# Splitting the first scan projection's weights one stage earlier, in a diffusion backbone kernel on one core

## The chip, the cores and the metric

The kernel runs on one core of a Trainium2 chip, as one program. The metric is the device time of one execution in microseconds, smaller is better. The core has a matrix engine (PE, with its weight loads shown as PEld), a vector engine (DVE), a scalar engine (ACT) and a general engine (POOL), and queues that issue DMA transfers; nearly all of this kernel's are issued from SP.

## The reference

Two layers over 1024 latent tokens and 256 context tokens, model width 1024, all in float32. The even layer mixes by pooling and short convolutions. The odd layer has two branches of width 512: a bidirectional RWKV-7 scan over 8 heads of 64 and a Conformer convolution. The part in question:

```python
def odd_merge(y_c, z_c, p1, p2, z_d, w_out, dw_w, dw_b, ln_g, ln_b, grid):
    y_d = conformer_branch(p1, p2, dw_w, dw_b, ln_g, ln_b, "cols" if grid else "seq")
    y = jnp.concatenate([y_c * jax.nn.silu(z_c), y_d * jax.nn.silu(z_d)], axis=-1)
    return y @ w_out

def wkv_scan(r, w, k, v, a, bb, s0, reverse):
    def step(s, inp):
        r_t, w_t, k_t, v_t, a_t, b_t = inp
        sa = jnp.einsum("bhvk,bhk->bhv", s, a_t)
        s = s * w_t[:, :, None, :] + sa[..., None] * b_t[:, :, None, :] + v_t[..., None] * k_t[:, :, None, :]
        return s, jnp.einsum("bhvk,bhk->bhv", s, r_t)
```

The inputs of both branches and their gates (`r`, `k`, `v`, `z_c`, `p1`, `p2`, `z_d`) are column blocks of one projection, `h @ w_in`, of the modulated and normalised stream. Of these `p1`, `p2` and `z_d` aren't needed by the recurrence.

## The kernel before

**Split products.** A float32 value is kept as a rounded high half and a low half (value minus high half). A product of two such matrices is three matmuls into the same PSUM bank: low weights by high data, high by low, high by high. A weight tile of 128 x 1024 arrives raw by DMA in the one raw buffer `wr`; a cast on ACT makes the high half `wh`, a subtract the low half `wl`. There are two pairs of `wh` and `wl`, one in the pool `wp` and one in the pool `wpb`, used in turn by `(n - i) % 2` for the i-th tile of a list of n = 52 tiles.

**Stages.** `layer_even` is the even layer and its output projection. `odd_in` prepares the scan: it runs the projections for `r`, `k`, `v` of four head pairs j and four gate projections (matmuls at L1016), and works decay, keys and so on out of them on DVE, ACT and POOL; the results go to DRAM (`ARD`, `BKD`, `BTD`, `VTD`, `GD`, `ZCD`, ...). Here the low halves come by DMA from DRAM (`LOD`, made in the even layer), the high halves by a cast at L998. A gate projection's output is multiplied by `GD` at L1061 and stored to `ZCD` at L1063. `scan` does the recurrence in chunks of 64 tokens: 20 groups, each with key products (L1522) from `w` and `bk`, which DMAs at L1498 and L1505 bring in, inverses of small triangular blocks on POOL (L1420, L1421), and a chain of 40 dependent steps (L1741 on PE). Between these, as fill for PE, stand the remaining 12 projections (L1960, 48 matmuls each, 576 in all) and the output projection (L2102, 288 and L2307, 144 matmuls).

**Order.** The class `Lists` walks jobs (Python generators) that yield the engine and a planned duration of their next piece, or a resource or an event to wait for, and takes among those that are due the one with the best priority. It runs when the program is built; what comes out is a fixed order on each engine and in SP's queue, and on the chip each engine works through its list in that order, waiting on semaphores. So a job that becomes due at another time can reorder all later work. `odd_in` and `scan` each have their own such plan, one after the other.

**The first scan projection's weights.** In `odd_in`, `weights` (L980) loads tile after tile into `wr` and, for i < n, spawns `split_w` (L990), which takes the resource `w0` or `w1` (a free pair), has the low half loaded, casts the high half and frees `wr`. For i = n the tile is the first one of the scan, `self.wfirst`: it is loaded, and stays raw. In `scan`, `weights` (L1907) and `split_w` (L1920) go over the 12 projections and the output tiles: take `wr`, load (not for i = 0), then for each half of the tile cast on ACT (L1928) and subtract on DVE (L1934), then free `wr`, which lets the next tile's load be issued. The scan starts on the pair in `wp`; a second pair comes free much later.

```python
            for i, src in enumerate(self.worder):
                yield "R", "wr"
                at = L.got
                if i == 0:
                    raw = self.wfirst
```

Of the kernel before, what the change touches and what calls it, by code (L numbers as in the profile page):

```python
# [8 lines left out]
F32 = mybir.dt.float32  # L9
F32R = mybir.dt.float32r  # L10
AF = mybir.ActivationFunctionType
ALU = mybir.AluOpType
# [84 lines left out]
class Lists:  # L97
# [13 lines left out]
    def spawn(self, gen, prio):  # L111
        e = Job(gen, prio, self.cur.ready if self.cur else 0.0)
        self.advance(e)
        self.jobs.append(e)
        return e
# [6 lines left out]
    def note(self, key):  # L122
        self.ev[key] = self.cur.ready

    def free(self, name, what=None):
        self.res[name].append((self.cur.ready, what))
# [53 lines left out]
class Kern:  # L180
# [14 lines left out]
               wr=[0.0], w00=[0.0], w10=[0.0], w01=[], w11=[])  # L195
# [712 lines left out]
    def odd_in(self, es):  # L908
        tc, nc, A = self.tc, self.nc, self.A
# [67 lines left out]
        L = Lists(self.SL, self.LAT, self.RES2)  # L977
        spawn, note, free = L.spawn, L.note, L.free

        def weights():  # L980

            for i in range(i0 + 1, n + 1):
                if i > i0 + 1:
                    yield "R", "wr"
                    yield "S", 600, 3700
                    self.load(i)
                if i < n:
                    spawn(split_w(i), self.WP)

        def split_w(i):  # L990
            yield "R", f"w{(n - i) % 2}"
            p = (self.wp, self.wpb)[(n - i) % 2]
            raw = self.raws.pop(i)
            self.ready[i] = hi, lo = [p.tile([128, 8, 128], F32R, tag=t, name=t) for t in ("wh", "wl")]
            yield "S", 600, 300
            nc.sync.dma_start(out=lo.bitcast(F32), in_=self.LOD[i - n])
            yield "A", 950, 3100
            nc.scalar.copy(hi, raw)  # L998
            free("wr")
            note(("w", i))  # L1000
        used = [len(self.order) - self.NZ - 3 * NJ]
# [425 lines left out]
    def scan(self, es):  # L1427
# [454 lines left out]
        def rhs(src, k, b, c0, n):  # L1882
            return hn[src, k, b][:, c0:c0 + n]

        wts = [[[t[:, :4], t[:, 4:]] for t in (self.wp.tile([128, 8, 128], F32R, tag=t, name=t) for t in ("wh", "wl"))]]
        place = []

        def wt(a, k, ahead=0):
# [18 lines left out]
        def weights():  # L1907

            for i, src in enumerate(self.worder):
                yield "R", "wr"  # L1910
                at = L.got
                if i == 0:
                    raw = self.wfirst
                else:
                    raw = at or self.wp.tile([128, 8, 128], F32, tag="wr", name="wr")
                    yield "S", 600, 3700
                    self.wload(raw, src)
                spawn(split_w(i, raw, at), self.WP)

        def split_w(i, raw, at):  # L1920
            if i:
                yield "E", ("w", i - 1, 1)
            place.append((1 - place[-1]) if i and L.res["w01"] + L.res["w11"] + [1] * (1 in place) else 0)
            for q in range(2):
                yield "R", f"w{q}{place[i]}"
                (hi, lo), r = (t[q] for t in wts[place[i]]), raw[:, 4 * q:4 * q + 4]
                yield "A", 530
                nc.scalar.copy(hi, r)  # L1928
                if i < self.LOG:
                    yield "G", 1150  # L1930
                    nc.gpsimd.tensor_tensor(out=lo, in0=r, in1=hi.bitcast(F32), op=ALU.subtract)
                else:
                    yield "D", 610
                    nc.vector.tensor_tensor(out=lo, in0=r, in1=hi.bitcast(F32), op=ALU.subtract)  # L1934
                if q:
                    free("wr", at)
                note(("w", i, q))
# [485 lines left out]
```

## Time and profile before

| What | Value |
|---|---|
| Time, median of 3 runs | 1552.14 us (1549.43 to 1553.41) |
| Profiled execution, its own time | 1545.31 us |
| Its span in the profile | 1543.5 us |
| Granted TensorE clock, mean | 0.951 of full speed |
| Busy: PE, DVE, POOL, ACT | 1381.1, 993.9, 671.9, 637.0 us |

The busy times are those of one profiled execution; an engine counts as busy while it executes, not while it waits for a semaphore. The timelines give for each instruction its start from the span's start, its duration, its line and tiles, and in brackets how long its engine had been idle before it and what ended that. The chain of waits is followed back from the last instruction and names at each moment the work that the end was waiting for.

### The profile page before, as it was taken

The page shows a single profiled execution, that of the slowest core. Times are in us where ns is not written, and L with a number is a line of the kernel's source. Part 1 is how long each engine was busy: PE and PEld are TensorE (multiplying, and loading weights), DVE is VectorE, ACT ScalarE, POOL GpSimd, SP SyncE. Part 2 cuts the span into 40 slices and gives each one's busy share as a digit, 9 for nine tenths or more (in the row PEclk, how much of TensorE's full clock was granted, in tenths as well). Part 3 has the DMA queues.
Part 4 walks back from the last instruction along what each step waited for, and adds up shares of the span by engine and source line. Part 5 has one row for each costly group of instructions (what it writes and reads, how often), then busy time and mean ns, then how long its engine had stood idle before and what let it go on. Part 6 is the DMA issues. An engine that isn't in the chain of part 4 may idle for free.

```text
span 1543.5 us, 32203 instructions
## 1 busy us (share of the span) xinstructions
PE 1381.1 (89%) x12820; PEld 1084.7 (70%) x12820; DVE 993.9 (64%) x1681; ACT 637.0 (41%) x1257; POOL 671.9 (44%) x925
## 2 busy tenths in 40 slices
PE   6899999998999999899889878888998988886996
PEld 1578788887888778677667656676776666764775
DVE  3744464545822561279999964778688777788567
ACT  2551112122322552356556531344445643657534
POOL 1343535548455532135545421755557246406003
PEclk9899999999999999999999989899998998898999
DMA  7413433634253210537657775655655566774223
GB/s 266 152 66 123 169 131 129 213 137 162 70 174 124 67 65 33 147 99 218 199 169 226 224 253 150 159 141 150 168 141 151 165 157 173 218 225 127 86 86 109
DMA packets 174374, 232.32 MB, mean 151 GB/s; under 512 B 38832, under 2 KB 130352, under 8 KB 174096
## 3 DMA queue, kind: packets, MB, share of 16 engines
q1 hardware_dynamic: 172928, 228.69, 48.7%
q8 instruction: 101, 1.65, 0.5%
q10 hardware_dynamic: 1296, 1.57, 0.3%
q14 instruction: 49, 0.40, 0.1%
HBM read 164.93 MB, written 63.31 MB: 148 GB/s over the span
## 4 chain that ended last, share of the span: by engine, by line
PE 49%; DVE 17%; DMA 11%; POOL 10%; issue 6%; ACT 5%; SPq 2%; DVEq 0%; POOLq 0%; ACTq 0%
PE d L302 25%; PE d L2102 3%; PE d L1960 3%; PE d L1016 3%; DMA Bc<-ED 2%; POOL X L1421 2%; POOL tmp L1420 2%; DMA bk<-BKD 2%; PE sc L1522 2%; PE d L944 2%; DMA ad<-in_ada_e 1%; POOL wl L268 1%; PE pa L1741 1%; PE pr L458 1%; DVE Z L1090 1%
## 5 line engine op out<-in xcount | busy, mean ns | idle before, releaser
L302 PE MATMUL d<-sx,wh 128*128 128x512 f32 x1152 | 365.8, 399 | 2.4 <-DVE sx L528 1.3
L302 PEld LDWEIGHTS d<-sx,wh 128*128 128x128 f32 x1152 | 220.5, 192 | 54.2 <-POOL sx L398 1.8
L302 PE MATMUL d<-sx,wl 128*128 128x512 f32 x576 | 233.1, 405 | 12.3 <-POOL wl L268 9.1
L1420 POOL TENSOR_TENSOR tmp<-X,Bc 128x120 f32<-128x120 f32 (+2 forms) x300 | 120.0, 400 | 195.0 <-DMA Bc<-ED 172.6
L1016 PE MATMUL d<-sx,wh 128*128 128x512 f32 x512 | 162.8, 400 | 0.0
L268 POOL TENSOR_TENSOR wl<-wr,wh 128x1024 fp32r<-128x1024 f32 x37 | 98.8, 2671 | 139.4 <-ACT wh L267 139.4
L629 DVE SCALAR_TENSOR_TENSOR junk<-wra,cb 128x1024 bf16<-128x1024 f32 x56 | 108.3, 1934 | 75.5 <-DMA wra<-in_ada_o 51.0
L1960 PE MATMUL d<-sx,wh 128*128 128x512 f32 x384 | 139.3, 430 | 0.0
L302 PEld LDWEIGHTS d<-sx,wl 128*128 128x128 f32 x576 | 110.4, 192 | 38.7 <-POOL wl L268 10.1
L1421 POOL TENSOR_TENSOR X<-X,tmp 128x120 f32<-128x120 f32 (+2 forms) x300 | 124.8, 416 | 23.5
L1016 PEld LDWEIGHTS d<-sx,wh 128*128 128x128 f32 x512 | 98.6, 193 | 22.1 <-issue 2.7
L1016 PE MATMUL d<-sx,wl 128*128 128x512 f32 x256 | 112.9, 441 | 0.0
L302 PE MATMUL d<-sc,wh 128*128 128x256 f32 x576 | 104.1, 281 | 0.0
L1960 PE MATMUL d<-sx,wl 128*128 128x512 f32 x192 | 83.8, 437 | 9.8 <-DVE wl L1934 9.8
L1981 DVE SCALAR_TENSOR_TENSOR acc<-hc,vec,acc 128x960 f32<-128x960 f32 (+14 forms) x120 | 90.0, 774 | 1.1
L302 PEld LDWEIGHTS d<-sc,wh 128*128 128x128 f32 x576 | 88.8, 190 | 1.4
L267 ACT CAST wh<-wr 128x1024 fp32r<-128x1024 f32 x37 | 38.7, 1046 | 119.8 <-PE d L302 64.5
L1960 PEld LDWEIGHTS d<-sx,wh 128*128 128x128 f32 x384 | 74.5, 200 | 16.5 <-issue 0.2
L302 PE MATMUL d<-sc,wl 128*128 128x256 f32 x288 | 81.0, 281 | 0.0
L1522 PE MATMUL sc<-w,bk 64*128 64x128 f32 (+1 forms) x640 | 55.4, 311 | 20.4 <-issue 9.1
L1522 PEld LDWEIGHTS sc<-w,bk 64*128 64x128 f32 x640 | 46.8, 210 | 28.2 <-issue 25.2
L1536 DVE TENSOR_TENSOR w<-sc,cstb 64x256 f32<-64x256 f32 x80 | 33.8, 422 | 47.2 <-PE sc L1522 28.5
(381 smaller groups left out, 2880.6 us busy)
## 6 DMA issues: line engine op xcount, KB each, us to landing
wr<-in_in_o SPq DMA_DIRECT2D x32, 512.0 KB
wr<-in_in_e SPq DMA_DIRECT2D x24, 512.0 KB
wra<-in_ada_o SPq DMA_DIRECT2D x24, 512.0 KB
BKD<-bk SPq DMA_DIRECT2D x40, 256.0 KB
BTD<-X SPq DMA_DIRECT2D x20, 512.0 KB
bk<-BKD SPq DMA_DIRECT2D x40, 256.0 KB
Bc<-ED SPq DMA_DIRECT2D x20, 512.0 KB
bkt<-BTD SPq DMA_DIRECT2D x40, 256.0 KB
```

Source lines behind the costliest of these rows:

```text
L267: self.nc.scalar.copy(hi, raw)
L268: self.nc.gpsimd.tensor_tensor(out=lo, in0=raw, in1=hi.bitcast(F32), op=ALU.subtract)
L302: self.nc.tensor.matmul(ps[:, :n], lhsT=w[a][:, k, :], rhs=rhs(src, k, b, c0, n), start=(i == 0), stop=(i == len(seq) - 1))
L629: nc.vector.scalar_tensor_tensor(out=junk, in0=w, scalar=1.0, in1=cb[:, s, :], op0=ALU.mult, op1=ALU.mult, accum_out=dst[:, s:s + 1])
L1016: nc.tensor.matmul(ps, lhsT=w[a][:, k, :], rhs=rhs(s, k, b, c0, m), start=(q == 0), stop=(q == len(seq) - 1))
L1420: g.tensor_tensor(out=t, in0=X[:, :, j:j + 1].to_broadcast([128, 8, m]), in1=B[:, j, :, j + 1:16] if j < 8 else B2[:, j - 8, :, j - 7:8], ...
L1421: g.tensor_tensor(out=X[:, :, j + 1:16], in0=X[:, :, j + 1:16], in1=t, op=ALU.add)
L1522: nc.tensor.matmul(ps[h][:, d, i, h:h + 1] if ctx else ps[h][:, d, i], lhsT=bk[R[h], c, d, i], rhs=w[R[h], c, d, sl, i, :], start=True, st ...
L1536: nc.vector.tensor_tensor(out=w[o, c, :, 2 * h], in0=ps[h][o, :, :, h], in1=ma[o].unsqueeze(2).to_broadcast([64, 2, 2, 64]), op=ALU.mult)
L1960: nc.tensor.matmul(ps, lhsT=wt(a, k), rhs=rhs("x", k, b, c0, 512), start=(i == 0), stop=(i == len(seq) - 1))
L1981: nc.vector.scalar_tensor_tensor(out=acc[:, o], in0=hc[:, q], scalar=w, in1=acc[:, o], op0=ALU.mult, op1=ALU.add)
L2102: nc.tensor.matmul(ps, lhsT=wt(a, at), rhs=ysrc(k, b, c0), start=(i == 0), stop=(i == len(seq) - 1))
```

## The change

`split_w` in `odd_in` now also runs for i = n: it waits for the pair of buffers in `wp` that the last but one gate projection frees, casts the whole tile on ACT, and subtracts on POOL (there is no stored low half for this tile); `wr` is free after that. In `scan`, the first pair of `wts` is that tile's. For i = 0, `weights` takes no `wr` and `split_w` only notes that the halves are there. Thus the two ACT casts of half a tile, and the two DVE subtracts, of the first scan projection are gone from the scan, and the raw buffer is free when its plan begins.

```diff
@@ odd_in @@
-                if i < n:
-                    spawn(split_w(i), self.WP)
+                spawn(split_w(i), self.WP)
 
         def split_w(i):
+
             yield "R", f"w{(n - i) % 2}"
             p = (self.wp, self.wpb)[(n - i) % 2]
             raw = self.raws.pop(i)
             self.ready[i] = hi, lo = [p.tile([128, 8, 128], F32R, tag=t, name=t) for t in ("wh", "wl")]
-            yield "S", 600, 300
-            nc.sync.dma_start(out=lo.bitcast(F32), in_=self.LOD[i - n])
+            if i < n:
+                yield "S", 600, 300
+                nc.sync.dma_start(out=lo.bitcast(F32), in_=self.LOD[i - n])
             yield "A", 950, 3100
             nc.scalar.copy(hi, raw)
+            if i == n:
+                yield "G", 2310
+                nc.gpsimd.tensor_tensor(out=lo, in0=raw, in1=hi.bitcast(F32), op=ALU.subtract)
             free("wr")
             note(("w", i))
@@ scan @@
-        wts = [[[t[:, :4], t[:, 4:]] for t in (self.wp.tile([128, 8, 128], F32R, tag=t, name=t) for t in ("wh", "wl"))]]
+        wts = [[[t[:, :4], t[:, 4:]] for t in self.ready[len(self.order)]]]
@@ scan, weights @@
             for i, src in enumerate(self.worder):
-                yield "R", "wr"
-                at = L.got
-                if i == 0:
-                    raw = self.wfirst
-                else:
+                raw = at = None
+                if i:
+                    yield "R", "wr"
+                    at = L.got
                     raw = at or self.wp.tile([128, 8, 128], F32, tag="wr", name="wr")
                     yield "S", 600, 3700
                     self.wload(raw, src)
@@ scan, split_w @@
             for q in range(2):
                 yield "R", f"w{q}{place[i]}"
+                if i == 0:
+                    note(("w", i, q))
+                    continue
                 (hi, lo), r = (t[q] for t in wts[place[i]]), raw[:, 4 * q:4 * q + 4]
```

The engines' orders move as follows; the new lines of the changed kernel lie 4 to 6 lines lower than the old ones (L1960 is now L1966, L1934 is L1940, L1498 is L1502, L1505 is L1509). Numbers behind a tile's name are versions of it; `w` and `bk` are operands of the key products, `sx` the halves of the input stream, `wh` and `wl` the weight halves.

On PE, where the preparation's last matmuls end and the scan's first projection begins, before:

```order
L1016 MATMUL d<-sx_131,wl 128x512
L1016 MATMUL d<-sx_132,wh 128x512
L1016 MATMUL d<-sx_131,wh 128x512
L1960 MATMUL d<-sx_117,wl 128x512 [waits DVE_49]
L1960 MATMUL d<-sx_118,wh 128x512 [waits Activation_49]
L1960 MATMUL d<-sx_117,wh 128x512
L1960 MATMUL d<-sx_119,wl 128x512
```

and the same place now:

```order
L1020 MATMUL d<-sx_131,wl 128x512
L1020 MATMUL d<-sx_132,wh 128x512
L1020 MATMUL d<-sx_131,wh 128x512
L1966 MATMUL d<-sx_117,wl 128x512 [waits DVE_49,Pool_49]
L1966 MATMUL d<-sx_118,wh 128x512
L1966 MATMUL d<-sx_117,wh 128x512
L1966 MATMUL d<-sx_119,wl 128x512
```

The first matmul's DVE semaphore stood before for the low half's subtract; now it stands for the eviction L1051 (now L1055) of the last preparation bank, and the POOL semaphore for the new subtract. The waits for halves inside the first 48 matmuls are gone. The 32 fill matmuls that stood ahead of the key products of group 0 are now 60, the 76 ahead of those of group 1 now 100, the 116 ahead of group 2 now 144, the 160 ahead of the chain's first step 188; at the chain's step 30 all 576 have been issued in both, and 303 fill matmuls follow the chain's last step instead of 297.

On SP's queue at the start of the scan, before:

```order
L1441 DMA cstb<-in_cstb 128x408
L1498 DMA w_7354<-ARD 64x128 x8
L294 DMA wr<-in_in_o 128x1024
L1505 DMA bk<-BKD 128x2x256 x2
L1498 DMA w_7355<-ARD 64x128 x8
L1498 DMA w_7356<-ARD 64x2x128 x8
L1571 DMA ED_7334<-eb 128x128
L1571 DMA ED_7335<-eb 128x64
L1505 DMA bk<-BKD 128x2x256 x2
```

and now:

```order
L1445 DMA cstb<-in_cstb 128x408
L294 DMA wr<-in_in_o 128x1024
L1502 DMA w_7357<-ARD 64x128 x8
L1502 DMA w_7358<-ARD 64x128 x8
L1509 DMA bk<-BKD 128x2x256 x2
L1502 DMA w_7359<-ARD 64x2x128 x8
L294 DMA wr<-in_in_o 128x1024
L1502 DMA w_7360<-ARD 64x2x128 x8
L1575 DMA ED_7338<-eb 128x128
L1575 DMA ED_7339<-eb 128x64
L1509 DMA bk<-BKD 128x2x256 x2
```

The raw load of the second projection's weights is now the first after `cstb`; group 0's `bk` stands behind the `w` transfers of two groups instead of one, and group 1's `bk` behind one more raw load and eight more `w` transfers.

On DVE, between the chain's steps 35 and 36, on the way to the subtract of a late weight tile, before:

```order
L2180 SCALAR_TENSOR_TENSOR stat<-part,stat 128x256
L1846 TENSOR_TENSOR sq<-sq,ms 128x256
L1848 SCALAR_TENSOR_TENSOR rs<-sq,rs 128x256
L2188 TENSOR_TENSOR cv<-cv,stat 128x512
L1859 SCALAR_TENSOR_TENSOR dv<-dv,vec,rs 128x256
L2188 TENSOR_TENSOR cv<-cv,stat 128x512
L2166 TENSOR_TENSOR stat<-part 128x256
L1863 SCALAR_TENSOR_TENSOR dv<-dv,vec,ms 128x256
L1865 TENSOR_TENSOR dv<-dv,sq 128x256
L1934 TENSOR_TENSOR wl<-wr,wh 128x512
```

and now:

```order
L2181 TENSOR_TENSOR stat<-stat,part 128x256
L2165 SCALAR_TENSOR_TENSOR cv<-d,cv 128x512 x2
L1940 TENSOR_TENSOR wl<-wr,wh 128x512
L2185 TENSOR_TENSOR part<-part,stat 128x256
L2186 SCALAR_TENSOR_TENSOR stat<-part,stat 128x256
L2194 TENSOR_TENSOR cv<-cv,stat 128x512
L1846 TENSOR_TENSOR ms<-ms,sq 128x256
L2194 TENSOR_TENSOR cv<-cv,stat 128x512
```

The subtract of the second half stood behind the norm operations of the scan's and the convolution's output (`rs`, `dv`, `cv`); it now stands ahead of most of them. On ACT the casts of half a tile fall from 32 to 30, those of a whole tile at L998 (now L999) rise from 15 to 16, and there are four activation table loads more (one each at L1835, L2018, L2170 and L2192). On POOL the one new row, the subtract, stands behind the last `kd` product (L1215) and ahead of the copies to `PT` (L1235). The counts on PE and SP are the same in both.

## Rows read from the trace of the kernel before

**Rows 1.** The page's first part: busy us, share of span, instructions.
```profile
PE 1381.1 (89%) x12820; PEld 1084.7 (70%) x12820; DVE 993.9 (64%) x1681; ACT 637.0 (41%) x1257; POOL 671.9 (44%) x925
```

**Rows 2.** Timeline of PE: start us, us, what, count, [idle before <-releaser].
```profile
913.37 0.63 PE L1016 MATMUL d<-sx,wh 128*128 128x512 f32 x2
923.59 0.79 PE L1960 MATMUL d<-sx,wl 128*128 128x512 f32 x1 [9.59 <-DVE wl L1934]
...
927.25 0.39 PE L1960 MATMUL d<-sx,wl 128*128 128x512 f32 x1
...
932.01 0.39 PE L1960 MATMUL d<-sx,wl 128*128 128x512 f32 x1
...
934.35 0.66 PE L1522 MATMUL sc<-w,bk 64*128 64x64 f32 x8 [0.15 <-DMA bk<-BKD]
```

**Rows 3.** Timeline of DVE, the same stretch.
```profile
907.91 1.23 DVE L1061 TENSOR_TENSOR ex<-ex 128x1024 f32<-128x1024 f32 x1 [2.59 <-DMA ex<-GD]
...
914.66 0.69 DVE L1051 SCALAR_TENSOR_TENSOR ex<-ex,d 128x512 f32<-128x512 f32 x1 [0.90 <-ACT ex L1049]
920.80 1.23 DVE L1061 TENSOR_TENSOR ex<-ex 128x1024 f32<-128x1024 f32 x1 [5.45 <-DMA ex<-GD]
...
922.87 1.27 DVE L1934 TENSOR_TENSOR wl<-wr,wh 128x512 fp32r<-128x512 f32 x2
```

**Rows 4.** Timeline of SP's queue at the scan's start: time to issue.
```profile
922.47 0.38 SPq L1441 DMA_DIRECT2D cstb<-in_cstb  x1
923.08 5.11 SPq L1498 DMA_DIRECT2D w<-ARD  x8
928.29 0.53 SPq L294 DMA_DIRECT2D wr<-in_in_o  x1
928.86 0.94 SPq L1505 DMA_DIRECT2D bk<-BKD  x2
929.85 10.15 SPq L1498 DMA_DIRECT2D w<-ARD  x16
```

**Rows 5.** Chain of waits, transfers on it: start us, us to landing, what.
```profile
915.67 5.04 DMA ex<-GD
...
929.34 4.97 DMA bk<-BKD
...
942.80 7.12 DMA wr<-in_in_o
...
1275.15 2.10 DMA sv<-VTD
```

**Rows 6.** Timelines of ACT and POOL in the preparation.
```profile
886.70 1.06 ACT L998 CAST wh<-wr 128x1024 fp32r<-128x1024 f32 x1
...
900.88 0.59 ACT L1330 COPY X<-t 128x512 f32<-128x512 f32 x1 [0.89 <-DMA BTD<-X]
...
909.64 1.27 POOL L1256 TENSOR_TENSOR kb<-kd 128x256 f32<-128x256 f32 x1 [3.12 <-DMA BON<-kb]
```

**Rows 7.** The page's costliest groups: busy us, mean ns | idle before.
```profile
L268 POOL TENSOR_TENSOR wl<-wr,wh 128x1024 fp32r<-128x1024 f32 x37 | 98.8, 2671 | 139.4 <-ACT wh L267 139.4
```

**Rows 8.** Windows: us, each engine's busy us, then PEclk, DMA share, GB/s.
```profile
923.60:927.30 3.70, 3.70 (x10) 2.93 (x11) 0.53 (x1) 0.00 (x0) 0.29 (x1) 0.56 0.53 158
988.00:1316.50 328.50, 290.33 (x5840) 225.62 (x5840) 250.83 (x560) 152.36 (x383) 185.38 (x471) 0.93 0.60 156
1378.00:1416.00 38.00, 25.59 (x340) 18.00 (x341) 31.50 (x67) 23.95 (x55) 22.60 (x55) 0.87 0.48 140
```

**Rows 9.** Timelines of PE and DVE late in the scan.
```profile
1402.54 0.79 PE L2102 MATMUL d<-y,wl 128*128 128x512 f32 x1 [8.63 <-DVE wl L1934]
...
1393.48 0.41 DVE L1842 TENSOR_TENSOR ms<-ms,sq 128x256 f32<-128x256 f32 x1
...
1401.77 0.71 DVE L1934 TENSOR_TENSOR wl<-wr,wh 128x512 fp32r<-128x512 f32 x1
```

**Rows 10.** Groups kept apart by shape: busy us, mean ns | idle before.
```profile
L1835 ACT ACT_TABLE_LOAD x5 | 6.4, 1283 | 0.1
```

## Prediction, made blind

> **What bounds the kernel now.** I began with the busy shares: TensorE (PE) works 89% of the span [rows 1], so a microsecond in which PE stands still, with work left that only it can do, is a microsecond of the end unless a chain of dependences ends it later. Next I read PE's timeline where the preparation of the scan ends and the scan begins [rows 2]. The last matmul of the preparation starts at 913.37, and the scan's first matmul at 923.59, after 9.59 us of idling until a low half of the weights (`wl`, L1934) is there. VectorE's (DVE) timeline says why it is late [rows 3]: the subtract that makes it is at 922.87, behind the last gate multiply L1061 at 920.80, which waits 5.45 us for a load of `GD`; that load leaves SP's queue at 915.67 and takes 5.04 us [rows 5]. The weights themselves have long been in the raw buffer. So the first projection is held by its place in DVE's order, and by nothing that it needs.
>
> SP's queue is the second thing to see [rows 4]. After `cstb` at 922.47 it issues the eight `w` transfers of key group 0 (5.11 us for eight issues), then the second projection's raw weights, then the two `bk` transfers; the second `bk` leaves at 929.34 and takes 4.97 us to land [rows 5], and the first key products run at 934.35 [rows 2]. From 988, where the chain of the groups has begun, to 1316.5 PE is busy 290.33 of 328.50 us [rows 8], some 88%: neither full, which would make every earlier microsecond count, nor idle enough for the chain alone to set the pace. That is the doubt of this forecast.
>
> **The change part by part.** The profiled execution took 1545.31 us (span 1543.5); the median is 1552.14, 0.44% above. I sum differences against the profile and put them on the median.
>
> *1. The gap.* The first projection's pair is ready in the preparation. In the changed order its first matmul waits for the last eviction of the preparation (L1051) and for the new POOL subtract; the eviction is at 914.66 and lasts 0.69 us, with 0.05 to start: PE starts at 915.4 instead of 923.59, **−8.2 us**. After the gap PE's first matmuls are slow: ten start between 923.59 and 927.25, in 3.66 us, nine intervals of 0.407 us, while the 21 intervals to 932.01 take 4.76 us, 0.227 each [rows 2]; the granted clock there is 0.56 of full speed [rows 8], about the lower level (1.2 of 2.4 GHz). With PE idle for 1.8 us instead of 9.6 I take these nine at 0.227: 9 × 0.18 = **−1.6 us**.
>
> *2. The next weights.* First projection: 48 × 0.227 = 10.9 us, so it ends at 926.3. The second one's raw weights are issued once `cstb` is, at about 922.9 instead of 928.29, and land 5.04 to 7.12 us later (the shortest and longest 512 KB transfer on the chain) [rows 5], at 927.9 to 930.0; half a cast, about 0.6, and a subtract of 0.7 [rows 9] give 929.3 to 931.4. PE waits 3.0 to 5.1 us there: a **new wait**, which takes some of the gap's gain back. Then twelve matmuls (2.7 us) to at most 934.1, about 932 at the early end.
>
> *3. The keys of group 0.* The same order puts one raw load and sixteen `w` issues ahead of the two `bk`: 922.9 + 0.53 + 10.15 [rows 4] + 0.5 = 934.1 for the second `bk`, instead of 929.34, 4.8 us later. Landing by the row of 4.97 gives 939.1, by the shortest row of a small transfer (2.10, `sv`) [rows 5] 936.2; I take 4.97, which is the same transfer. The first key products then come 4.75 us later (939.1 against 934.35), but with 60 fill matmuls behind them instead of 32: 28 × 0.227 = 6.4 us of work done. Net −1.6. PE has nothing else there, so it idles some 5 us before them and may drop to the lower clock again: up to +1.6 back, which leaves 0.
>
> The Trainium skill ("DMA: Bandwidth & Descriptors", section "Anatomy of one DMA — SWDGE (gpsimd) path") gives a transfer a fixed cost of about 2.0 us plus its bytes at 436 GB/s; that page fits it for transfers issued from GpSimd, these leave SP's queue. As an estimate by that page 256 KB take 2.6 us, the keys would come 2.4 us late, and the net would be −4.0; the trace's row for this transfer is nearly twice that, and it decides.
>
> *4. Groups 1 and 2.* Group 1's keys have one raw load and eight `w` more ahead (0.53 + 5.11 = 5.6 us [rows 4]) against 24 fills done earlier (5.4): +0.2. Group 2's: 5.6 later against 28 fills (6.4): −0.8. The mean of the three, (−1.6 + 0.2 − 0.8)/3 = **−0.7 us**, is my value for the start. Its ends: −9.8 (terms 1 and 1b kept whole, the chain never late) and +5.6 (the chain of groups sets the pace, each comes by what SP is later, and the fills done ahead buy nothing).
>
> *5. The fill runs out earlier or not.* In the changed order PE has 28 fills more behind it at chain step 0, 12 to 20 at steps 18 to 21, none at step 30, where all 576 are done in both. The lead is thus spent within the chain: fewer fills stand between its steps. It is a gain where PE is the later one, and idle time where the chain is. The 88% above [rows 8] fit both, so I take the middle, that is, term 4 as it stands.
>
> *6. Late in the scan.* PE waits 8.63 us, to 1402.54, for a `wl` whose subtract stands at 1401.77, behind a row of norm operations on DVE that began at 1393.48 [rows 9]. The changed order puts that subtract ahead of most of them: −8.6 at best, if nothing follows that is as late; PE is busy 25.59 of 38.00 us there [rows 8], so something else is late too, and six fills more remain after the last chain step (6 × 0.227 = +1.4). On the other side the order holds four ACT table loads more; such a load takes 1283 ns [rows 10]: +5.1 if each lies on the path. Middle of −8.6 and +5.1: **−1.75 us**.
>
> *7. What lies under cover.* The new whole cast on ACT (1.06 [rows 6]) comes where ACT has 0.89 of idle ahead of L1330 [rows 6]; what is left, 0.2, meets DVE's 2.59 before L1061 [rows 3]. The new POOL subtract takes 2.67 us (same form [rows 7]) and stands ahead of the operations that lead to 909.64, where POOL idles 3.12 [rows 6]; without that cover it would cost up to 2.7 through the keys of the last preparation. The two DVE subtracts and two ACT casts that go (1.27 on DVE [rows 3]) end nothing by themselves.
>
> Sum: −0.7 − 1.75 = −2.5 us; on the median 1552.14 − 2.5 = 1549.6, put at **1549.5 us**.
>
> **The rivals.** *A, little is left (my forecast):* as above; within ±4.66 us of the median (0.3%, about what a measurement of this kernel can tell from no change). For it: terms 2 and 3, a wait for weights and one for `bk` where there was one gap. That PE doesn't start early at all (the POOL subtract not done by 915.4) also ends here, near 1552.
>
> *B, the lead survives:* the 28 fills count whole, 6.4 us, or all of term 1, 9.8: 1552.1 − 6.4 to − 9.8 − (0 to 1.75) = 1540.6 to 1545.7, and down to 1534 if term 6 gives its 8.6 too. For it: PE's 89% [rows 1]. Against: 38 us of idling from 988 on [rows 8], which says that fills alone don't fill the chain.
>
> *C, slower:* SP's queue decides. Each early group's `bk` stands behind more `w` issues (0.63 each), the chain of groups is the later one from group 0 on, and starts 4.75 to 5.6 us later with nothing to make it good; then 1556.9 to 1557.7, with the table loads (+5.1) up to 1562.8. It decides as soon as PE's idling between the chain's steps grows by more than the 6.4 us of fill that it no longer has to do there. For it: the keys already wait for `bk` before [rows 2].
>
> **How the numbers follow.** A 0.40, B 0.37, C 0.23: A because the two new waits each take back a known share; B before C because PE's share is high and the fills done early are real work. The time is A's, 1549.5. The range takes in most of B (to 1541.0) and of C (to 1559.0) and leaves about 0.1 out on each side; A's own range is 1547.5 to 1556.8. Faster by over 0.3% is B, slower is C.
>
> **What would show it.** Term 1: the first L1960 matmul (a few lines lower in the new code) at 915 to 916, and no run of 0.4 us intervals behind it. Term 2: a PE wait of 3 to 5 us for `wl` after 48 matmuls. Term 3: the first key products at 936 to 940, with PE idle ahead of them for `bk`. Terms 4 and 5: the chain's first step no earlier than 986, and PE's idle time between steps larger than before by about the start's gain. Term 6: no 8.63 us wait near 1400, and ACT table loads on the chain of waits. The forecast is wrong if the chain's first step comes 6 us or more earlier and stays so (B), or later than 992 (C).

## The result and the profile after

The changed kernel is slower: 1558.11 us, median of 19 runs (1544.20 to 1571.17), against 1549.61 for the kernel before in the same comparison. The ratio is 1.0055, interval 1.0039 to 1.0072: 8.5 us lost, where 2.5 us were forecast to be gained. Single executions lie up to 14 us from their kernel's median (the one profiled of after took 1563.56, that of before 1545.31), so the 18.25 us between the two profiled ones overstate the loss; what follows rests on places that come back in several traces.

Up to the first keys the start went much as worked out. PE's timeline of after (start us, us, instruction, [idle before <-what ended it]), against [rows 2]:

```profile
913.02 0.63 PE L1020 MATMUL d<-sx,wh 128*128 128x512 f32 x2
915.14 0.47 PE L1966 MATMUL d<-sx,wl 128*128 128x512 f32 x1 [1.50 <-DVE ex L1055]
...
928.46 0.50 PE L1966 MATMUL d<-sx,wl 128*128 128x512 f32 x1 [2.17 <-DVE wl L1940]
...
937.01 1.12 PE L1526 MATMUL sc<-w,bk 64*128 64x64 f32 x8 [4.07 <-issue]
938.34 1.12 PE L1526 MATMUL sc<-w,bk 64*128 64x64 f32 x8 [0.21 <-DMA bk<-BKD]
...
991.60 1.06 PE L1745 MATMUL pa<-sv,w 128*64 128x64 f32 x16
```

PE starts at 915.14 instead of 923.59, waits 2.17 us for the next weights, and stands idle again ahead of the first keys, whose second eight run at 938.34 instead of 934.35, and take 1.12 us instead of 0.66. The last row is the chain's step 0: 991.60, later than before, although 28 fill matmuls more have been done. The same row of the kernel before:

```profile
987.89 0.69 PE L1741 MATMUL pa<-sv,w 128*64 128x64 f32 x16
```

SP's queue of after at the scan's start, against [rows 4]:

```profile
921.95 0.38 SPq L1445 DMA_DIRECT2D cstb<-in_cstb  x1
922.39 0.77 SPq L294 DMA_DIRECT2D wr<-in_in_o  x1
923.38 10.07 SPq L1502 DMA_DIRECT2D w<-ARD  x16
933.50 1.10 SPq L1509 DMA_DIRECT2D bk<-BKD  x2
...
947.54 0.81 SPq L1575 DMA_DIRECT2D ED<-eb  x2
...
955.34 1.36 SPq L1582 DMA_DIRECT2D Bc<-ED  x2
```

The last row, `Bc`, is the load from which POOL makes the first inverses. It left at 950.55 before:

```profile
950.55 1.33 SPq L1578 DMA_DIRECT2D Bc<-ED  x2
```

Later in the scan, the waits view of PE (what waited for what: us in total, times, longest), first of before from step 0 on:

```profile
PE d L2102 <- DVE wl L1934: 8.6, 1, 8.6
...
PE pa L1746 <- DVE rh L1743: 4.1, 6, 1.4
...
PE d L2152 <- DVE stat L2149: 0.5, 2, 0.2
```

and of after:

```profile
PE pa L1750 <- DVE rh L1747: 13.9, 7, 5.0
...
PE d L2158 <- DVE stat L2155: 10.4, 2, 9.9
```

The late wait for `wl` [rows 9] is gone, as the order had said; two others stand in its place: for `rh` (the chain's own copy out of PSUM, queued on DVE behind other work) and for `stat`. The windows (us, busy PE, PEld, DVE, ACT, POOL, then the granted clock) from step 0 to the end, of before and of after:

```profile
987.90:1543.50 555.60, 473.38 (x8053) 366.59 (x8052) 414.20 (x888) 274.81 (x656) 240.89 (x585) 0.92 0.54 151
```

```profile
991.60:1561.50 569.90, 470.24 (x8026) 365.42 (x8024) 406.28 (x877) 280.48 (x661) 237.65 (x586) 0.89 0.51 146
```

PE is without work for 82.2 us of the one and 99.7 of the other, and its matmuls, 27 fewer, take nearly as long at the lower granted clock. That PE idles more comes back in the other traces: 80.7 to 87.9 us from step 0 on in the eight of the old order that leave out no matmul behind step 0 (before, b2, e1, e6, e9, e11, e12, e16), 88.9 to 99.7 in the six of the changed one (after, e2, e3, e4, e13, e15), 11 us more in the mean.

### The profile page after: what moved, and what is told of

Its sections match the earlier page's. It is cut to its first block, busy times and chain, and to the rows that moved or that the text cites. A ratio compares the mean times of both kernels' runs of the same rounds, so it can differ in the third digit from the quotient of the medians.

```text
span 1561.5 us, 32197 instructions
## 1 busy us (share of the span) xinstructions
PE 1385.8 (89%) x12820; PEld 1091.0 (70%) x12820; DVE 998.6 (64%) x1679; ACT 641.9 (41%) x1260; POOL 666.8 (43%) x926
## 4 chain that ended last, share of the span: by engine, by line
PE 49%; DVE 16%; DMA 11%; POOL 9%; issue 7%; ACT 6%; SPq 3%; DVEq 0%; POOLq 0%; ACTq 0%
PE d L302 24%; PE d L1966 4%; PE d L1020 4%; DMA Bc<-ED 3%; PE d L2108 3%; POOL tmp L1424 2%; POOL X L1425 2%; PE d L944 2%; PE sc L1526 1%; POOL wl L268 1%; DMA cv<-CVD 1%; PE pa L1769 1%; DMA ad<-in_ada_e 1%; PE pa L1750 1%; DVE acc L1987 1%
## 5 line engine op out<-in xcount | busy, mean ns | idle before, releaser
L629 DVE SCALAR_TENSOR_TENSOR junk<-wra,cb 128x1024 bf16<-128x1024 f32 x56 | 113.2, 2021 | 73.9 <-DMA wra<-in_ada_o 49.1
L1966 PE MATMUL d<-sx,wh 128*128 128x512 f32 x384 | 142.0, 441 | 0.0
L1425 POOL TENSOR_TENSOR X<-X,tmp 128x120 f32<-128x120 f32 (+2 forms) x300 | 119.5, 398 | 23.5
L1020 PEld LDWEIGHTS d<-sx,wh 128*128 128x128 f32 x512 | 99.7, 195 | 22.2 <-issue 2.7
L302 PEld LDWEIGHTS d<-sc,wh 128*128 128x128 f32 x576 | 88.9, 190 | 1.4
L1966 PE MATMUL d<-sx,wl 128*128 128x512 f32 x192 | 85.6, 446 | 3.7 <-DVE wl L1940 2.2
L1966 PEld LDWEIGHTS d<-sx,wh 128*128 128x128 f32 x384 | 76.6, 206 | 16.8 <-issue 0.4
L267 ACT CAST wh<-wr 128x1024 fp32r<-128x1024 f32 x37 | 38.7, 1047 | 120.6 <-PE d L302 72.2
L1219 POOL TENSOR_TENSOR kd<-kd,Z 128x512 f32<-128x512 f32 x20 | 29.5, 1477 | 77.7 <-DVE kd L1215 77.7
```

The costliest lines, as they stand in the source:

```text
L267: self.nc.scalar.copy(hi, raw)
L302: self.nc.tensor.matmul(ps[:, :n], lhsT=w[a][:, k, :], rhs=rhs(src, k, b, c0, n), start=(i == 0), stop=(i == len(seq) - 1))
L629: nc.vector.scalar_tensor_tensor(out=junk, in0=w, scalar=1.0, in1=cb[:, s, :], op0=ALU.mult, op1=ALU.mult, accum_out=dst[:, s:s + 1])
L1020: nc.tensor.matmul(ps, lhsT=w[a][:, k, :], rhs=rhs(s, k, b, c0, m), start=(q == 0), stop=(q == len(seq) - 1))
L1425: g.tensor_tensor(out=X[:, :, j + 1:16], in0=X[:, :, j + 1:16], in1=t, op=ALU.add)
L1966: nc.tensor.matmul(ps, lhsT=wt(a, k), rhs=rhs("x", k, b, c0, 512), start=(i == 0), stop=(i == len(seq) - 1))
```

## The experiments

Each run has its own trace. Ratios are to the kernel before, measured beside it. The third column is step 0's start less that of the preparation's last matmul row, in us (that row itself starts anywhere from 910.1 to 916.8 in these traces); the fourth is step 0's start less the issue of the first `Bc`.

| Run | Ratio (95%) | Step 0 after preparation | after first `Bc` |
|---|---|---|---|
| before, first trace | 1 | 74.5 | 37.3 |
| b2_before_again | 1.0002 (0.9982 to 1.0021) | 72.2 | 36.6 |
| the changed kernel | 1.0055 (1.0039 to 1.0072) | 78.6 | 36.3 |
| e1_early_old_plan | 1.0041 (1.0024 to 1.0058) | 77.1 | 38.6 |
| e2_late_new_plan | 1.0049 (1.0030 to 1.0069) | 79.7 | 37.3 |
| e3_bk0_first | 1.0047 (1.0028 to 1.0066) | 77.4 | 37.2 |
| e4_ed0_first | 1.0047 (1.0027 to 1.0066) | 79.5 | 38.0 |
| e6_bk0_late | 1.0026 (1.0006 to 1.0046) | 80.2 | 37.6 |
| e7_fill_less | 1.0012 (0.9996 to 1.0027) | 74.2 | 37.4 |
| e9_zcd_off_sp | 1.0001 (0.9982 to 1.0020) | 69.8 | 36.7 |
| e11_gap_kept_busy | 1.0023 (1.0003 to 1.0044) | 73.8 | 37.6 |
| e12_zcd_off_sp_late | 1.0005 (0.9989 to 1.0021) | 70.8 | 36.3 |
| e13_after_zcd_off_sp | 1.0030 (1.0004 to 1.0055) | 76.3 | 37.8 |
| e14_zcd_off_sp_sw51 | 0.9992 (0.9974 to 1.0010) | 71.9 | 36.7 |
| e15_after_less_ahead | 1.0053 (1.0029 to 1.0077) | 76.6 | 36.9 |
| e16_before_less_ahead | 1.0004 (0.9985 to 1.0022) | 72.9 | 36.3 |
| jb1_before_c608 | 1.0130 (1.0098 to 1.0162) | 73.5 | 37.8 |
| jb2_before_sw51 | 0.9993 (0.9974 to 1.0012) | 72.4 | 36.8 |
| ja1_after_c612 | 1.0110 (1.0079 to 1.0141) | 79.2 | 36.9 |
| ja2_after_sw51 | 1.0103 (1.0064 to 1.0141) | 79.5 | 37.1 |

### The two halves of the change, each alone

**e1_early_old_plan** is the changed kernel with the old pieces kept in the scan's plan, so that the order stays (shown is `split_w`; in `weights` it also takes `wr` for i = 0, as before):

```diff
+                if i == 0:
+                    yield "A", 530
+                    yield "D", 610
+                    if q:
+                        free("wr", at)
+                    note(("w", i, q))
+                    continue
```

> The weights of the first scan projection are split in the preparation as in the changed kernel, but the scan's plan still holds the old pieces for them (two casts, two subtracts, the raw buffer's release at the old moment) without issuing them, so every engine and SP's queue keep the order of the kernel before. PE can start at 915 but stands after 32 fill matmuls, at 922.7, before key products whose bk lands at 934.3 as before. Theory Q (SP's queue brings the first groups' bk 4 to 5 us later and the chain never makes it good): 1549 to 1550 us, the same as before. Theory O (the new interleaving of fill and chain inside the scan costs the time, whatever the start): 1549 to 1550 as well, at best 1548. If the early split itself costs (the cast on ACT, the subtract on POOL ahead of the last keys): 1551 to 1553.

**e2_late_new_plan** is the kernel before, its casts and subtracts issued at the plan's start without pieces of their own, so that the plan is the changed one (shown is `split_w`; in `weights` the take of `wr` for i = 0 is gone):

```diff
+                if i == 0:
+                    nc.scalar.copy(hi, r)
+                    nc.vector.tensor_tensor(out=lo, in0=r, in1=hi.bitcast(F32), op=ALU.subtract)
+                    note(("w", i, q))
+                    continue
```

> The other half of the pair: the first projection's weights are split in the scan as in the kernel before (casts on ACT, subtracts on DVE at the head of the scan), but the scan's plan is that of the changed kernel, so PE, DVE, ACT, POOL and SP have its order. PE starts at 923.6 again, and its 60 fills ahead of the first keys end near 938 to 940 instead of waiting for bk. Theory Q: the keys come at 939 to 943, as in the changed kernel or up to 4 us later: 1557 to 1562 us. Theory O: the plan costs as much as in the changed kernel or more, since the earlier start's gain is gone: 1558 to 1564. If the early split itself is what costs: 1549 to 1552.

Both lose: 1.0041 (1554.73 us) and 1.0049 (1557.55). Each half costs about 0.4 to 0.5%, and the two together 0.55%, so they don't add. That the early split costs something with the order held was only the last and least of the expectations for it.

### What SP's queue does to the start

**e3_bk0_first** and **e4_ed0_first** move transfers in the changed kernel's queue, **e6_bk0_late** one in that of the kernel before. In the expectations theories Q and P say that a late start of the chain is carried to the end, O that the time is lost between the chain's steps, D that it is lost by a lower granted clock:

```diff
 e3: changed kernel, in group(G), right behind its w
+            if G == 0:
+                (the two bk transfers of group 0)
 e4: as e3, and
+            if G == 3:
+                late.append(bring)          (its w, issued behind the ED store of group 0)
 e6: kernel before
+            if G == 0:
+                late.append(bring)          (its bk, issued behind the w of group 1)
```

> The changed kernel with one thing moved: the two bk transfers of group 0 are issued right after group 0's own eight w transfers instead of after group 1's, so they leave SP's queue some 5 us earlier; no engine's order changes. The first keys then come at about 934 instead of 938.3. Theory Q: the 4 us come back, 1553 to 1555 us. Theory O: group 0's keys are ahead of need, and what is lost is lost between the chain's steps: 1557 to 1559.

> The changed kernel with SP's queue put back at the scan's start: group 0's bk is issued right after its own w, and group 3's eight w are issued after group 0's ED store (the store of the blocks that the first inverses on POOL need) instead of ahead of it; no engine's order changes. ED of group 0 leaves at about 941 instead of 947.5, as in the kernel before. Theory P: the first inverses and chain step 0 come 4 us earlier, and that is carried to the end: 1553 to 1555 us. Theory D: the start doesn't matter, 1556 to 1559.

> The kernel before with one thing moved: group 0's two bk transfers are issued after group 1's eight w transfers, 5.1 us later; no engine's order changes. First keys at about 939.4 instead of 934.35, and PE idles that much longer. Theory Q: 1553 to 1555 us, slower by most of the 5 us. Theory O: 1549 to 1551.5, made good within the chain.

Delaying `bk` in the kernel before costs 0.26% (1553.17 us), the least that Q had expected. Its timeline of SP and of PE:

```profile
954.94 1.33 SPq L1588 DMA_DIRECT2D Bc<-ED  x2
```

```profile
992.58 0.69 PE L1751 MATMUL pa<-sv,w 128*64 128x64 f32 x16
```

`Bc` leaves 4.4 us later than in the first trace of before, and step 0 comes 4.7 later. In the changed kernel the two moves bring next to nothing (both 1.0047, within the interval of 1.0055). The timelines of DVE and SP of e3 say why for the first:

```profile
937.43 1.13 DVE L1578 SCALAR_TENSOR_TENSOR eb<-e,cstb,eb 128x128 f32<-128x128 f32 x3
```

```profile
946.04 1.01 SPq L1583 DMA_DIRECT2D ED<-eb  x2
```

With its `bk` early, `eb`, the operand of the inverses that DVE makes from the keys, is there at 938.56, but its store `ED` stands in the queue behind `w` and a raw load and leaves 7.5 us later. The queue of e4 says it for the second: counted from the preparation's last matmul, `ED` leaves 6 us earlier than in the changed kernel, but `Bc`, behind two groups of `w`, a `bk` and a raw load, only 0.7 us:

```profile
939.28 0.85 SPq L1591 DMA_DIRECT2D ED<-eb  x2
940.18 5.13 SPq L1506 DMA_DIRECT2D w<-ARD  x8
945.41 1.05 SPq L1525 DMA_DIRECT2D bk<-BKD  x2
946.51 5.13 SPq L1506 DMA_DIRECT2D w<-ARD  x8
952.05 0.35 SPq L294 DMA_DIRECT2D wr<-in_in_o  x1
952.46 1.36 SPq L1600 DMA_DIRECT2D Bc<-ED  x2
```

So e4 was no clean test of the start: it moved `ED` and not the load that counts. The table's last column shows which counts: in 20 traces step 0 comes 36.3 to 38.6 us after the first `Bc` is issued, whatever stands in PE's order by then.

### What fill done ahead is worth

**b2_before_again** is the kernel before once more. **e7_fill_less** takes 32 fill matmuls out between steps 0 and 30, **e15_after_less_ahead** and **e16_before_less_ahead** take 30 out ahead of step 0:

```diff
 e7
+                    if a == 0 or k not in (3, 5) or used[0] < 4:
 e15, e16
+                    if a == 0 or k not in (1, 3, 4, 5, 6) or used[0] > 2:
                         nc.tensor.matmul(ps, lhsT=wt(a, k), ...
```

> The kernel before once more, unchanged: a second trace and the granted clock of each of its runs. 1548.6 us, ratio 1.000 within 0.2%. Theory P (the chain of groups sets the pace, a late start of it is carried to the end): chain step 0 at 987 to 989 as in the first trace. Theory D (the changed kernel loses to a lower granted clock, through the places where PE idles): mean granted clock of its runs about 0.949, against 0.944 to 0.945 in the changed kernel and in the early split alone.

> The kernel before without 32 of the 576 fill matmuls: in the fifth to twelfth projection the product of low data and high weights is left out for two of the eight blocks (those outputs lose a low-order part); all lie between the chain's steps 0 and 30, 32 x 0.227 = 7.3 us of PE work. It measures what fill done ahead is worth there. If PE's work sets the pace: 1541 to 1542 us. Theory P: 1547 to 1549, little or nothing. Theory D: fewer fills make PE idle more and the clock lower, 1548 to 1551.

> The changed kernel without 30 fill matmuls ahead of the chain's first step: in the first three projections the product of low data and high weights is left out for five of the eight blocks (those outputs lose a low-order part). 30 x 0.227 = 6.8 us of PE work, so about as many fills stand ahead of step 0 as in the order before. Theory F (the fills put ahead hold the first groups back, PE being in order, and buy nothing later): step 0 at 985 to 988 instead of 991.6, and the time 1552 to 1555 us. If the start is set elsewhere (SP's queue, the inverses on POOL): step 0 at 990 to 992 and 1556 to 1559.

> The same 30 matmuls left out of the kernel before. There the first 32 fills end ahead of the landing of bk, which sets the first keys. Theory F: step 0 at 983 to 987 instead of 988, since the later groups' fills shrink too; the time 1545 to 1549 us. If the start is set elsewhere: 1548 to 1550.

None of the three cuts gains: 1.0012, 1.0053 against the changed kernel's 1.0055, 1.0004. Some 7 us of PE's work, taken out, are worth nothing that can be told at the end, at either place: e7's interval allows a gain of 0.6 us at most, e16's of 2.3. (The matmuls left out are those of low weights by high data, the first of the three products, not low data by high weights as the expectations say; the count is the same.) e15 also speaks against the theory that it was run for, that the fills put ahead hold the first groups back in PE's order: without 30 of them step 0 comes at 991.24, where 985 to 988 were expected, and 76.6 after the preparation, not 73.

### The early split's own cost

**e9_zcd_off_sp** is e1 with the last ZCD store on ACT's queue, **e12_zcd_off_sp_late** the kernel before with that store moved, **e13_after_zcd_off_sp** the changed kernel with it, **e14_zcd_off_sp_sw51** e9 with `SW = 51`:

```diff
-            nc.sync.dma_start(out=self.ZCD[i], in_=z)
+            (nc.scalar if i == self.NZ - 1 else nc.sync).dma_start(out=self.ZCD[i], in_=z)
```

> The early split with the scan's old plan (as in the run before of that kind), and the last store of the preparation (ZCD, which waits for the last gate multiply at 922) issued from ACT's queue instead of SP's, so that cstb, w and bk of group 0 can leave SP from about 916 on instead of 922.5. Theory P: keys at 928, chain step 0 some 5 to 6 us earlier than with the early split alone, and all of it at the end: 1547 to 1549 us, against 1554.7. Theory D: PE no longer idles 10 us ahead of the first keys, so the clock stays up as well: 1545 to 1548. If what follows cstb waits for something else that comes at 922 anyway: 1554 to 1555.

> The kernel before with the last ZCD store issued from ACT's queue, and no early split: w and bk of group 0 can leave SP from about 916, but the scan's first matmul still waits for the DVE subtract behind L1061, and the keys stand behind 32 fills: they come at about 932 to 933, 2 us earlier than before. If the early split costs nothing by itself: 1547 to 1549 us, 0 to 2 below the kernel before and no better than with the early split (1549.8). If the early split costs some 4 to 6 us by itself: 1543 to 1545.

> The changed kernel with the last ZCD store issued from ACT's queue; no engine's order changes but for that store. SP's queue starts the scan 6 us earlier, the second projection's weights and group 0's bk with it: no wait of PE after 48 matmuls, first keys at about 932 instead of 938, chain step 0 at 985 to 987 instead of 991. If an early start of the chain is carried to the end under this order: 1552 to 1554 us. If the new order eats it: 1556 to 1558.

> Early split with the old pieces held in the scan's plan, the last ZCD store issued from ACT's queue, and the allowance of fill 51 instead of 50 (the order that cost nothing with the late split, 1548.65 us). If gains add: 1543 to 1547. If the start is worth nothing under this order either: 1548 to 1551.

**e11_gap_kept_busy** is e1 with a matmul repeated in PE's gap:

```diff
+                    for _ in range(45 if (used[0], c0, i) == (0, 512, 7) else 1):
                         nc.tensor.matmul(ps, lhsT=wt(a, k), ...
```

> The early split with the scan's old plan, and one matmul of the first projection repeated 44 times just ahead of the first key products (its output is off by the repeated terms): 44 x 0.227 = 10 us of PE work in the 10.3 us gap that PE has there. Theory K (that gap lets the granted clock fall, and the keys and the fills after them run at the lower clock): with PE busy the key products take 0.66 us per eight instead of 1.0, chain step 0 comes at 988 instead of 990.6, and the time falls from 1554.7 to 1549 to 1552. If something else of the early split costs: 1554 to 1556.

With the store off SP, the early split costs nothing (e9 1.0001, e1 1.0041), and the changed kernel measures 1.0030, with an interval that overlaps that of 1.0055 (1555.59 us, between its two expectations). e12, without the early split, stays at 1.0005 (1550.84 us, above both of its expectations, as e9 is 0.8 us above what P had expected): the split itself neither gains nor costs once the queue is free. In e1 the gap of 9.59 us has only moved, to the place ahead of the first keys; timeline of e1, then of e11:

```profile
933.46 1.97 PE L1526 MATMUL sc<-w,bk 64*128 64x64 f32 x16 [10.27 <-issue]
```

```profile
932.66 1.26 PE L1526 MATMUL sc<-w,bk 64*128 64x64 f32 x16 [0.28 <-issue]
```

Before, the first projection's matmuls ran at the lower clock behind the gap [rows 2, 8], and the keys, which count, at the full one. In e1 the sixteen keys take 1.97 us; with PE kept busy 1.26. The windows behind it (granted clock third from the end), e1 and e11:

```profile
934.00:960.00 26.00, 26.00 (x136) 20.81 (x135) 9.46 (x22) 5.90 (x13) 0.83 (x2) 0.81 0.49 128
```

```profile
934.00:960.00 26.00, 23.53 (x132) 18.24 (x132) 14.53 (x28) 5.91 (x13) 3.94 (x4) 1.00 0.55 139
```

0.81 against 1.00, and step 0 at 77.1 against 73.8. In time it is 1.0041 against 1.0023: the direction that theory K wants, but the intervals overlap, and e11, at 1552.90 us between its two expectations, stays 0.0023 above the kernel before. So the clock's part at the start is shown in the trace, its price in the total only made likely. Over the whole span the clock doesn't tell the kernels apart as theory D wanted: the mean over a kernel's runs is 0.946 in b2 (0.949 was expected) and 0.945 in the changed kernel, but 0.942 in e16 and 0.944 in e7, which lose nothing.

### What another order costs

Four kernels change one number that only the planner reads, two of the kernel before and two of the changed one:

```diff
 jb1: -    C8 = 610    +    C8 = 608
 jb2: -    SW = 50     +    SW = 51
 ja1: -    C8 = 610    +    C8 = 612
 ja2: -    SW = 50     +    SW = 51
```

> The kernel before with one planned duration of the scan's chain pieces changed from 610 to 608 (a number that only the planner reads; no instruction is added or dropped but ACT table loads). The greedy plan comes out in another order: some 2160 of 8980 matmuls stand elsewhere, all after the scan has begun. Theory L (any new order of the scan costs, since the order before is a favourable one among many; the changed kernel loses because its plan was drawn anew): 1553 to 1560 us. Theory I (it is the early release of the raw buffer itself that gives a worse order): 1547 to 1551, like the kernel before.

> The same with another planned number: the allowance per group of four fill matmuls 51 instead of 50. Some 2500 of 8980 matmuls stand elsewhere. Theory L: 1553 to 1560 us. Theory I: 1547 to 1551.

> The changed kernel with the planned duration of the chain pieces 612 instead of 610: some 2120 of 8980 matmuls stand elsewhere than in the changed kernel. Theory L: anywhere between 1547 and 1562 us, not the 1558 of the changed kernel in particular. Theory I: 1556 to 1560 us again.

> The changed kernel with the planned allowance per group of four fill matmuls 51 instead of 50: some 830 of 8980 matmuls stand elsewhere. Theory L: anywhere between 1547 and 1562 us. Theory I: 1556 to 1560 us.

1568.14, 1548.65, 1564.29 and 1565.14 us; all but the second lie above even the ranges of theory L. A planned duration that is 0.3% shorter costs the kernel before 1.3%; another number leaves it where it is. The spread between orders is larger than the whole effect in question: the changed kernel's 0.55% lies inside it, and both of its neighbours are worse. That doesn't make the loss a mere draw: the three orders with the early release (after, ja1, ja2) all start the chain late (78.6 to 79.5) and all lose, of the three without it (before, jb1, jb2) one does. Whether the early release as such draws worse orders is too much to say from three and three. e14, which joins the early split, the free queue and the other order, is no faster than the kernel before (0.9992), so no version here beats it.

## Why the prediction was wrong

**Term 1** (the gap) held: 915.14 against 915.4 forecast, and no slow matmuls in the 48 behind it. They come later: behind the wait of term 2 PE's matmuls fall to 0.43 us apart from 930.18 on, and the first keys run slow, as term 3 had allowed for with up to 1.6 us. **Term 2** held in kind: a wait of 2.17 us, under the 3.0 to 5.1, since the raw weights landed 4.7 us after their issue (the cast behind them starts at 927.06). The 5.04 was not the shortest 512 KB transfer on the chain, as the term has it; one of `ad` takes 4.65. **Term 3** held: first keys at 938.34, 939.1 forecast. **Term 7** held: the last matmul row of the preparation starts at 913.0 in the mean of the eleven traces with the early split and at 913.2 in that of the nine without, so the new cast and subtract delay nothing there that can be told.

**The step that failed is the credit in terms 3 to 5:** 28 fills, 6.4 us of PE's work, set against keys 4.75 to 5.6 us late, which left −0.7. (That mean took −1.6 for group 0, although term 3 itself left 0 if the clock falls, and it fell.) The credit is worth nothing that these runs can tell. e7, e15 and e16 show it from three sides: fills can be taken away, ahead of the chain or within it, and the time stays. PE's 89% [rows 1] and its 88% within the chain [rows 8] had made me count half. What came in its place is idling: PE idles 11 us more from step 0 on, in the mean of the traces above, which is more than the 6.4 us of fill that it no longer has to do there. That was the condition named for rival C. The waits views put most of PE's waits to other engines and to loads; that fill in an order fixed beforehand doesn't shorten such waits is argued from e7, not shown wait by wait.

**What sets the start** is the late keys, carried on. I stopped at `bk` and the first keys. Behind them stand `eb`, its store `ED`, the load `Bc` and POOL's inverses. The second half of the keys, the operations of DVE that finish `eb`, the store, and POOL's first operation of the inverses, before:

```profile
936.98 1.11 PE L1522 MATMUL sc<-w,bk 64*128 64x64 f32 x16
939.75 1.12 DVE L1566 SCALAR_TENSOR_TENSOR eb<-e,cstb,eb 128x128 f32<-128x128 f32 x3
940.90 0.81 SPq L1571 DMA_DIRECT2D ED<-eb  x2
957.43 0.86 POOL L1420 TENSOR_TENSOR tmp<-X,Bc 128x120 f32<-128x120 f32 x1 [31.37 <-DMA Bc<-ED]
```

and after, where `ED` left at 947.54:

```profile
943.10 1.20 PE L1526 MATMUL sc<-w,bk 64*128 64x64 f32 x16
946.38 1.13 DVE L1570 SCALAR_TENSOR_TENSOR eb<-e,cstb,eb 128x128 f32<-128x128 f32 x3
962.97 0.49 POOL L1424 TENSOR_TENSOR tmp<-X,Bc 128x120 f32<-128x120 f32 x1 [37.11 <-DMA Bc<-ED]
```

In both `ED` leaves 0.03 us after `eb` is made (0.02 to 0.04 in 15 of the 20 traces): it waits for the keys. Those are 4.0 us late in their first half and 6.1 in their second, with fill at the lower clock between; from `ED` to `Bc` the changed queue takes 7.8 us instead of 9.65, so `Bc` leaves 4.8 us later. The queue alone would hold `ED` nearly as long, as e3 shows, so moving `bk` back is not enough. Step 0 comes 78.6 after the preparation, against 72.2 to 74.5 in the five traces with the old start (before, b2, e7, jb1, jb2): 4 to 6 us late.

That a late step 0 reaches the end is shown by e6, where one moved transfer makes it late and costs 4.0 us (interval 0.9 to 7.1), and by e1 against e9, where freeing the queue gives 0.40% back. Both also change how long PE idles ahead of the keys, and with it the clock; but e16 has the same mean clock as e6 from 910 to step 0 (0.79), no late step 0, and loses nothing. After against e13 points the same way (0.25%), with intervals that overlap.

This is rival C in its mechanism; it had 0.23. That its time fits too (1556.9 to 1557.7, with 1558.11 measured) is luck: C added 4.75 to 5.6 us to 1552.14, but the kernel before measured 1549.61 beside the changed one, so the loss is 8.5 us, and its sign, step 0 later than 992, was just not met (991.60). e6 prices a step 0 that comes later still (80.2) at 4.0 us. What is left of the 8.5 lies in the order within the scan, or in the two together; no run has the changed order with step 0 as early as before (e13 comes nearest, at 76.3).

**Term 6** was right about what goes and had no value for what comes. The 8.63 us wait is gone, in every trace of the new order. In its place: timeline of after on PE,

```profile
1356.73 1.22 PE L2158 MATMUL d<-stat,cstt 128*128 128x256 f32 x2 [9.88 <-DVE stat L2155]
```

on DVE,

```profile
1354.79 0.69 DVE L2161 TENSOR_TENSOR stat<-cv 128x512 f32<-128x512 f32 x1 [9.66 <-DMA cv<-CVD]
```

and on SP's queue,

```profile
1338.69 1.00 SPq L2150 DMA_DIRECT2D cv<-CVD  x2
```

DVE's next instruction in order needs a load issued 16 us earlier, and all that DVE holds for the chain waits behind it. In the six traces with the changed order at 610 and 50 (after, e2, e3, e4, e13, e15) PE waits 7.2 to 10.4 us for `stat` and 9.3 to 13.9 for `rh`; in the nine of the old order (before, b2, e1, e6, e7, e9, e11, e12, e16) 0.4 to 2.0 and 2.4 to 8.1, and 8.5 to 9.6 for the `wl` that the new order has done away with. So the new order has about 16 us more of such waits for 9 that it saves; some of the others, for `bk` above all, are shorter. But these waits don't tell a slow order from a fast one. The waits view of PE of jb2, which loses nothing:

```profile
PE d L2152 <- DVE stat L2149: 10.2, 3, 6.2
PE pa L1746 <- DVE rh L1743: 9.4, 7, 4.0
```

e14 has 8.8 and 10.8 and loses nothing either, while ja1, with 1.6 and 2.1, loses 1.1%. So what the two waits cost in the end is not shown; an earlier load of `CVD` was not tried. The table loads on ACT, my upper end for this term, stand among no waits of PE that I could find.

**What stays open.** A late step 0 costs, but an early one gains nothing: e9 and e12 start the chain some 3 us earlier than the kernel before (69.8 and 70.8 against 72.2 to 74.5) and end with it (1.0001, 1.0005). I know of no row that says where this goes. Nor is the part of the order within the scan split further: at about the same late start ja1 and ja2 lose about 5 parts in a thousand more than the changed kernel, and what in their orders does it was not looked for.

## What to carry to other kernels

Where a greedy plan sets the order, an edit that frees a resource earlier is two edits, the work saved and an order drawn anew; hold the old order (keep the planned pieces without issuing them) and try a few neighbours of a planner's number before giving the edit its credit or its blame. Follow a late start to the first step of the dependent chain through every engine and queue on the way, here keys, store, load and inverses, not only to the first wait that PE shows. Before a wait that is new in one trace gets the blame, look whether a version that loses nothing has it too. And test what a full-looking engine's work is worth by leaving some out: 32 matmuls fewer moved nothing here, at 89% busy.

## What the runs showed of the hardware

Two things I had not expected. An idle stretch of PE cost twice where it stood ahead of work that others wait for: the same sixteen key products took 1.97 us behind a 10.27 us gap and 1.26 behind none, with a granted clock of 0.81 against 1.00 over the next 26 us, so a gap that is moved, without being closed, can make the next step late; what of e1's 0.41% is due to it is not shown. And executions of one and the same kernel with one order spread by 21 us (1539.18 to 1559.92 in b2), and the two profiled ones, at 1559.92 and 1545.31 us, had mean granted clocks of 0.941 and 0.951, so a single trace against a single trace says little about 8 us.
